# First-layer expert weights in pieces of 512 rows by 512 columns, in a one-core layer with attention, a recurrence and 32 experts

## The chip, the cores and the metric

The kernel runs on one core of one Trainium2 chip. Five engines of the core appear in the profile: PE (TensorE, the matrix multiplier; PEld is its weight load, which overlaps the matmuls), DVE (VectorE), ACT (ScalarE), POOL (GpSimd) and SP (SyncE, which here only issues DMA transfers). The metric is the device time of one execution in microseconds (us); less is better.

## The reference, cut to what matters

One transformer layer on 1024 tokens of width 1024: a layer norm, a mixing block (latent attention beside a recurrence), another norm, and then a mixture of 32 experts, four per token. The change touches only the first matrix product of the experts.

```python
def clamped_swiglu(hh):
    x_glu = jnp.minimum(hh[..., ::2], SWIGLU_LIMIT)
    x_lin = jnp.clip(hh[..., 1::2], -SWIGLU_LIMIT, SWIGLU_LIMIT)
    return x_glu * jax.nn.sigmoid(SWIGLU_ALPHA * x_glu) * (x_lin + 1.0)

def expert_block(args):          # idx: the tokens of one expert e
    idx, e = args
    u = clamped_swiglu(h_pad[idx] @ w1[e] + b1[e])   # w1[e] is 1024 x 2048
    return u @ w2[e] + b2[e]                         # w2[e] is 1024 x 1024
```

The output of each expert is multiplied by the token's gate and added to the token's row.

## The kernel before

**Two kinds of experts.** The experts are ranked by their number of tokens, and each rank has a fixed capacity: 192, 184, 184, 176, 168, 160, 152, 152, 144, 144 and 136 slots for the eleven largest (the wide ones), and 128 for the other 21 (the narrow ones). They run in the order narrow, wide, narrow, wide, narrow, narrow, wide, narrow, narrow, wide and so on, so most of the program repeats a period of two narrow experts and one wide one.

**Three products for one.** Weights and activations are float32. Each is split into a rounded high part and a low part that holds the rest: an ACT cast writes the high part (`wsh`, L205), and a DVE subtraction writes the low part (`wsl`, L206). A product is then three matmuls in `mm`: high by high (L193), high part of the weights' side by low part of the other and the reverse (L194, L195).

**Pieces.** `piece` (L1378) loads 1 MB of weights as a tile of 128 partitions by 2048, by one DMA on SP's queue, and splits it in two halves of 1024 columns: two casts on ACT, and two subtractions on DVE. The loaded tiles `w` have five buffers, the split tiles `ws` four. One expert takes 12 pieces, eight for the first layer and four for the second. In the kernel before, a piece of the first layer holds all 1024 rows (eight blocks k of 128) of 256 columns.

**The narrow first layer** (`first`): the tokens `xT` stand on PE's stationary side, and the weights stream through. For each quarter q of the 2048 columns an accumulator `acc` of 128 x 512 gets a bias matmul (L1472) and then two pieces: piece j fills columns j * 256 to j * 256 + 255, by 8 blocks k of three matmuls of 256 columns each. Then ACT takes the sigmoid (L1482) and DVE the rest (L1484 to L1486).

**The wide first layer** (`first_wide`): here the weights are stationary, 128 x 128 at a time, and the tokens `xw` stream through. A group is one 128-column block of the weights, summed over k: for each k one matmul of the high part of the weights by high and low tokens side by side, 2 * cap columns (L1525), and one of the low part by the high tokens, cap columns (L1527). An expert has 16 groups, two per piece. A group's accumulator is drained by ACT (L1529: the half of the low tokens, plus the bias) and DVE (L1530: the sum of both halves). The drains are called T0 to T15 in what follows, and the subtractions of piece j are called S j. After each second group, ACT and DVE do the activation (L1534 to L1537) and split the result `u` for the second layer.

**Banks.** The accumulators `acc` rotate through four PSUM banks, so group g of a wide expert waits until the drain T(g-4) has emptied its bank.

**What sets the order.** The whole program is written in one pass, and a scheduler that simulates the engines puts each engine's instructions in a fixed order at build time. Each engine then runs its list strictly in that order, so an instruction that stands behind another one waits for it even if they have nothing to do with each other. The order of the matmuls of two groups can be interleaved by the scheduler.

## Time and profile before

| what | value |
|---|---|
| time, median of 3 runs | 2455.2 us (2453.6 to 2470.61) |
| time of the profiled execution | 2466.53 us |
| its span from first to last instruction | 2464.7 us |
| mean granted TensorE clock | 0.954 |
| PE busy over the span | 2286.7 us, 93% |
| DVE busy over the span | 1996.8 us, 81% |
| ACT busy over the span | 1409.1 us, 57% |
| DMA, mean over the span | 230 GB/s |

The rows that are shown below come from the profiled execution, which took 2466.53 us; its span, 2464.7 us, is what the trace covers. Times in the rows are microseconds from the start of the span. The experts run from 957 us to the end.

### The profile page before, as it was taken

Reading aid. Unit: us, or ns where it says so; the run is one execution under the profiler, and the core shown is the slowest. Engines: PE = TensorE matmul, PEld = TensorE weight load, DVE = VectorE, ACT = ScalarE, POOL = GpSimd, SP = SyncE. Lnnn points to the kernel's source line nnn. Section 1 sums busy time; section 2 is a strip of 40 time slices with the busy share of each in tenths; the row PEclk is TensorE's granted clock in tenths of the full one; section 3 lists DMA queues with packets and bytes.
Section 4 is the critical chain, followed back from the end, with each engine's and each line's share of the span. In section 5 each row is a group of like instructions: output and inputs, shape, how many; then the busy total and the mean of one; then the engine's idle time right before and its main releaser. Section 6 shows DMA issues by size and latency. Waiting matters only on the chain. (4 is left out here: it accounts for less than half of the span.)

```text
span 2464.7 us, 42046 instructions
## 1 busy us (share of the span) xinstructions
PE 2286.7 (93%) x15539; PEld 1940.2 (79%) x15539; DVE 1996.8 (81%) x3878; ACT 1409.1 (57%) x2355; POOL 549.3 (22%) x411
## 2 busy tenths in 40 slices
PE   6999989999998995899999999999999999999992
PEld 3776766676765784888898998989889898888981
DVE  7666447777776776788898989898989898898977
ACT  5333335455545433666676767676667676666764
POOL 1005222222213533121211212111212121111113
PEclk9999989999898995999999999999999999999996
DMA  6378542212123323978898979897979898888973
GB/s 268 119 263 278 187 112 56 59 45 58 34 41 90 115 96 128 342 283 290 297 335 296 338 288 337 281 358 275 363 252 336 297 334 302 292 326 300 333 272 139
DMA packets 167335, 567.80 MB, mean 230 GB/s; under 512 B 64617, under 2 KB 79738, under 8 KB 116821
## 3 DMA queue, kind: packets, MB, share of 16 engines
q1 hardware_dynamic: 155476, 524.63, 58.2%
q0 software_dynamic: 11216, 39.34, 6.5%
q8 instruction: 124, 2.03, 0.3%
q10 hardware_dynamic: 432, 1.09, 0.1%
q14 instruction: 87, 0.70, 0.1%
HBM read 508.22 MB, written 56.79 MB: 229 GB/s over the span
## 5 line engine op out<-in xcount | busy, mean ns | idle before, releaser
L206 DVE TENSOR_TENSOR wsl<-w,wsh 128x1024 fp32r<-128x1024 f32 x786 | 932.9, 1218 | 143.6 <-ACT wsh L205 142.1
L205 ACT CAST wsh<-w 128x1024 fp32r<-128x1024 f32 x786 | 782.8, 1047 | 346.6 <-PE acc L195 91.9
L193 PE MATMUL acc<-wsh,xTh 128*128 128x256 f32 x1344 | 381.9, 285 | 10.0 <-ACT xTh L205 5.1
L1525 PE MATMUL acc<-xw,wsh 128*128 128x368 f32 (+7 forms) x1408 | 381.1, 354 | 8.0 <-DVE t L1530 8.0
L194 PE MATMUL acc<-wsl,xTh 128*128 128x256 f32 x1344 | 382.9, 285 | 0.7 <-DVE wsl L206 0.7
L195 PE MATMUL acc<-wsh,xTl 128*128 128x256 f32 x1344 | 381.7, 285 | 0.3 <-DVE xTl L206 0.3
L1527 PE MATMUL acc<-xw,wsl 128*128 128x184 f32 (+7 forms) x1408 | 337.9, 240 | 0.0
L1525 PEld LDWEIGHTS acc<-xw,wsh 128*128 128x128 f32 x1408 | 268.9, 191 | 10.1 <-issue 5.4
L1527 PEld LDWEIGHTS acc<-xw,wsl 128*128 128x128 f32 x1408 | 273.3, 194 | 0.7
L193 PEld LDWEIGHTS acc<-wsh,xTh 128*128 128x128 f32 x1344 | 258.5, 193 | 13.2 <-ACT xTh L205 7.0
L194 PEld LDWEIGHTS acc<-wsl,xTh 128*128 128x128 f32 x1344 | 259.4, 193 | 4.8 <-DVE wsl L206 1.0
L195 PEld LDWEIGHTS acc<-wsh,xTl 128*128 128x128 f32 x1344 | 259.2, 193 | 1.8 <-DVE xTl L206 0.6
L1459 POOL DMA_INDIRECT y_d<-y,idx x42 | 143.0, 3405 | 420.5 <-DVE y L1451 333.3
L1362 POOL DMA_INDIRECT xg<-h_d,idx x43 | 97.7, 2273 | 615.7 <-issue 272.2
L193 PE MATMUL acc<-wsh,uTh 128*128 128x512 f32 x512 | 203.5, 400 | 19.2 <-ACT uTh L205 19.2
L194 PE MATMUL acc<-wsl,uTh 128*128 128x512 f32 x512 | 202.4, 396 | 0.0
L195 PE MATMUL acc<-wsh,uTl 128*128 128x512 f32 x512 | 193.6, 406 | 1.3 <-DVE uTl L206 1.3
L193 PEld LDWEIGHTS acc<-wsh,uTh 128*128 128x128 f32 x512 | 97.3, 190 | 40.7 <-ACT uTh L205 21.8
L193 PE MATMUL sm<-hTh,wsh 128*128 128x512 f32 x288 | 115.0, 400 | 6.4 <-ACT wsh L205 2.0
L194 PE MATMUL sm<-hTl,wsh 128*128 128x512 f32 x288 | 115.6, 401 | 4.2 <-DVE hTl L347 3.1
L195 PE MATMUL sm<-hTh,wsl 128*128 128x512 f32 x288 | 113.5, 395 | 0.0
L194 PEld LDWEIGHTS acc<-wsl,uTh 128*128 128x128 f32 x512 | 97.8, 191 | 19.3 <-DVE wsl L206 0.2
(584 smaller groups left out, 4323.5 us busy)
## 6 DMA issues: line engine op xcount, KB each, us to landing
w<-in_w_dram SPq DMA_DIRECT2D x384, 1024.0 KB
aw<-in_ada_dram SPq DMA_DIRECT2D x34, 512.0 KB
w<-in_w_in_dram SPq DMA_DIRECT2D x18, 512.0 KB
aw<-in_ada_dram SPq DMA_DIRECT2D x7, 1024.0 KB
rkv_d<-stage SPq DMA_DIRECT2D x12, 512.0 KB
xt<-in_x_dram SPq DMA_DIRECT2D x8, 512.0 KB
xr<-in_x_dram SPq DMA_DIRECT2D x8, 512.0 KB
xr_d<-xr SPq DMA_DIRECT2D x8, 512.0 KB
```

Source lines behind the costliest of these rows:

```text
L193: mm(out, a.hi, b.hi, start=start, stop=False)
L194: mm(out, a.hi, b.lo, start=False, stop=False)
L195: mm(out, a.lo, b.hi, start=False, stop=stop)
L205: (hi_eng or self.nc.scalar.copy)(dst.hi, src)
L206: (lo_eng or self.nc.vector).tensor_tensor(dst.lo, src, dst.hi.bitcast(F32), ALU.subtract)
L1362: self.nc.gpsimd.indirect_dma_start(out=xg[0:n], out_offset=None, in_=self.h2_d, in_offset=bass.IndirectOffsetOnAxis(ap=idx[0:n, 0:1], axi ...
L1459: nc.gpsimd.indirect_dma_start(out=self.y_d, out_offset=bass.IndirectOffsetOnAxis(ap=idx[0:n, 0:1], axis=0), in_=y[0:n], in_offset=None, c ...
L1525: nc.tensor.matmul(acc[:, 0:2 * cap], w.hi[:, c], xw[:, k].rearrange("p a t -> p (a t)"), start=(k == 0), stop=False)
L1527: nc.tensor.matmul(acc[:, 0:cap], w.lo[:, c], xw[:, k, 0], start=False, stop=(k == KD - 1))
```

## The change

The same 1 MB pieces of the first layer are cut another way: 512 rows (four blocks k) by 512 columns. The host's layout of `w1` follows, so that a piece is still one contiguous block.

- In the narrow first layer a quarter q still takes two pieces, but each piece m now adds four blocks k to all 512 columns of the accumulator: 12 matmuls of 512 columns per piece, where there were 24 of 256.
- In the wide first layer a group sums over all eight blocks k, so it needs both pieces of a pair. Two pieces are loaded and split together at every even j, and then the four column blocks of the pair are summed one by one, each over both pieces. The number and the sizes of the matmuls stay.

```diff
--- before.py
+++ after.py
@@ -140,8 +140,8 @@
     o["rw"] = f("router_w")[0].reshape(KD, P, NE).transpose(1, 0, 2)
     o["rb"] = f("router_b")
 
-    w1 = f("exp_w1")[0].reshape(NE, KD, P, 8, P, 2)
-    o["w1"] = w1.transpose(0, 3, 2, 1, 5, 4).reshape(NE, 8, P, KD, 256)
+    w1 = f("exp_w1")[0].reshape(NE, 2, 4, P, 4, 2, P, 2)
+    o["w1"] = w1.transpose(0, 4, 1, 3, 2, 5, 7, 6).reshape(NE, 8, P, 4, 512)
     o["w2"] = f("exp_w2")[0].reshape(NE, 4, 2, P, D).transpose(0, 1, 3, 2, 4)
     b1 = f("exp_b1")[0].reshape(NE, 8, P, 2).transpose(0, 1, 3, 2)
 
@@ -1470,12 +1470,11 @@
         for q in range(4):
             acc = pm.tile([P, 512], F32, name="acc", bufs=4)
             nc.tensor.matmul(acc, self.pick[:, q:q + 1].to_broadcast([P, P]), bs, start=True, stop=False)
-            for j in range(2):
-                ws = self.piece(w1[bass.ds(e, 1), 2 * q + j].rearrange("o p k n -> (o p) (k n)"))
-                for k in range(KD):
-                    w, c = ws[k // 4], k % 4 * 256
-                    self.mm(acc[:, j * 256:(j + 1) * 256], xT[:, k], w[:, c:c + 256],
-                            start=False, stop=(j == 1 and k == KD - 1))
+            for m in range(2):
+                ws = self.piece(w1[bass.ds(e, 1), 2 * q + m].rearrange("o p k n -> (o p) (k n)"))
+                for k in range(4):
+                    c = k % 2 * 512
+                    self.mm(acc, xT[:, 4 * m + k], ws[k // 2][:, c:c + 512], start=False, stop=(m == 1 and k == 3))
             a = acc.rearrange("p (j g f) -> p j g f", j=2, g=2)
             v2 = lambda t: t.rearrange("p (j f) -> p j f", j=2)
             sg = mp.tile([P, 256], F32, name="sg")
@@ -1515,13 +1514,17 @@
         n1 = cap - P
         w1 = self.i["w1"]
         for j in range(KD):
-            ws = self.piece(w1[bass.ds(e, 1), j].rearrange("o p k n -> (o p) (k n)"))
+            if j % 2 == 0:
+
+                ws = []
+                for m in range(2):
+                    ws += self.piece(w1[bass.ds(e, 1), j + m].rearrange("o p k n -> (o p) (k n)"))
             parts = []
             for g in range(2):
                 acc = pm.tile([P, 512], F32, name="acc", bufs=4)
+                a = j % 2 * 2 + g
                 for k in range(KD):
-                    w = ws[k // 4]
-                    c = slice(k % 4 * 256 + g * P, k % 4 * 256 + (g + 1) * P)
+                    w, c = ws[k // 2], slice(k % 2 * 512 + a * P, k % 2 * 512 + (a + 1) * P)
                     nc.tensor.matmul(acc[:, 0:2 * cap], w.hi[:, c], xw[:, k].rearrange("p a t -> p (a t)"),
                                      start=(k == 0), stop=False)
                     nc.tensor.matmul(acc[:, 0:cap], w.lo[:, c], xw[:, k, 0], start=False, stop=(k == KD - 1))
```

After the diff, lines from L1483 to L1485 on stand one line higher, and lines from L1520 on three lines lower: the wide matmuls L1525 and L1527 become L1528 and L1530, and the drains L1529 and L1530 become L1532 and L1533.

PE, the first quarter of a narrow expert's first layer, behind the end of the expert ahead of it (L1435 and L1439); `pick` and `bs1` are the operands of the bias. Before:

```order
L1439 MATMUL acc_13276<-wsl_13356,u1_8914 64x512
L1435 MATMUL acc_13276<-wsh_13355,u1_8914 128x512
L1472 MATMUL acc_13408<-bs1_8920,pick_8916 128x512
L193 MATMUL acc_13408<-wsh_13412,xTh_13238 128x256
L194 MATMUL acc_13408<-wsl_13413,xTh_13238 128x256
L195 MATMUL acc_13408<-wsh_13412,xTl_13239 128x256
L193 MATMUL acc_13408<-wsh_13412,xTh_13238 128x256
```

And now:

```order
L1439 MATMUL acc_12796<-wsl_12876,u1_8914 64x512
L1435 MATMUL acc_12796<-wsh_12875,u1_8914 128x512
L1472 MATMUL acc_12928<-bs1_8920,pick_8916 128x512
L193 MATMUL acc_12928<-wsh_12932,xTh_12758 128x512
L194 MATMUL acc_12928<-wsl_12933,xTh_12758 128x512
L195 MATMUL acc_12928<-wsh_12932,xTl_12759 128x512
L193 MATMUL acc_12928<-wsh_12932,xTh_12758 128x512
```

The bias matmul stays, and the three matmuls of a block k are twice as wide; a piece is used up after 12 matmuls, where it took 24.

DVE in the wide first layer of an expert with 152 slots: `wsl` is S (each row without x2 is one half of a piece), L1530 is T, L1535 to L1537 the activation, `uTl` and `u1` the splitting of its result. Before:

```order
L206 TENSOR_TENSOR wsl_20839<-w_20836,wsh_20838 128x1024
L1537 SCALAR_TENSOR_TENSOR t1_20596<-sg_20599,t1_20596 128x152
L206 TENSOR_TENSOR wsl_20839<-w_20836,wsh_20838 128x1024
L1530 TENSOR_TENSOR t1_20653<-acc_20636,t1_20653 128x152
L1530 TENSOR_TENSOR t0_20690<-acc_20673,t0_20690 128x152
L206 TENSOR_TENSOR uTl_20436<-t1_20596,uTh_20435 128x128
L206 TENSOR_TENSOR u1_8914<-t1_20596,u1_8914 128x24
L1535 TENSOR_SCALAR t1_20653<-t1_20653 128x152
```

And now, where T is L1533, from the end of the activation of groups 4 and 5 on (`x2` stands for both halves of a piece):

```order
L206 TENSOR_TENSOR u1_8914<-t1_19164,u1_8914 128x24
L206 TENSOR_TENSOR wsl_19342<-w_19339,wsh_19341 128x1024 x2
L206 TENSOR_TENSOR wsl_19350<-w_19347,wsh_19349 128x1024 x2
L1533 TENSOR_TENSOR t1_19213<-acc_19196,t1_19213 128x152
L1533 TENSOR_TENSOR t0_19258<-acc_19241,t0_19258 128x152
L1533 TENSOR_TENSOR t1_19278<-acc_19261,t1_19278 128x152
```

The last three rows are T7, T8 and T9. Further down DVE's list of the same expert, with the second layer's first two pieces as `wsl_19495` and `wsl_19515`:

```order
L1540 SCALAR_TENSOR_TENSOR t1_19278<-sg_19281,t1_19278 128x152
L206 TENSOR_TENSOR wsl_19495<-w_19492,wsh_19494 128x1024 x2
L1533 TENSOR_TENSOR t0_19307<-acc_19290,t0_19307 128x152
L206 TENSOR_TENSOR uTl_18996<-t1_19213,uTh_18995 128x128
L206 TENSOR_TENSOR u1_8914<-t1_19213,u1_8914 128x24
L206 TENSOR_TENSOR wsl_19515<-w_19512,wsh_19514 128x1024 x2
L206 TENSOR_TENSOR uTl_18996<-t1_19278,uTh_18995 128x128
L206 TENSOR_TENSOR u1_8914<-t1_19278,u1_8914 128x24
L1533 TENSOR_TENSOR t0_19372<-acc_19355,t0_19372 128x152
L1533 TENSOR_TENSOR t1_19327<-acc_19310,t1_19327 128x152
L1533 TENSOR_TENSOR t1_19392<-acc_19375,t1_19392 128x152
```

Before, one piece's two subtractions stand between two pairs of drains. Now four subtractions (S6 and S7) stand in front of the drain of the last group of a pair (`t1_19213`, which is T7). In front of T11 (`t1_19327`) stand four of the second layer, with T10 and T12 (`t0_19307`, `t0_19372`) between and behind them.

PE, the third group of the same expert. Before, groups 2 and 3 read one piece, `wsh_20496`; the rows in front of the first line are second-layer matmuls of the expert ahead:

```order
L195 MATMUL acc_20339<-wsh_20407,uTl_19986 128x512
L1525 MATMUL acc_20502<-xw_20290,wsh_20496 128x304
L1527 MATMUL acc_20502<-xw_20290,wsl_20497 128x152
L1525 MATMUL acc_20502<-xw_20290,wsh_20496 128x304
L1527 MATMUL acc_20502<-xw_20290,wsl_20497 128x152
```

And now, from the fourth block k on:

```order
L1528 MATMUL acc_19062<-xw_18850,wsh_18999 128x304
L1530 MATMUL acc_19062<-xw_18850,wsl_19000 128x152
L1528 MATMUL acc_19062<-xw_18850,wsh_19007 128x304
L1530 MATMUL acc_19062<-xw_18850,wsl_19008 128x152
L1528 MATMUL acc_19062<-xw_18850,wsh_19007 128x304
L1530 MATMUL acc_19062<-xw_18850,wsl_19008 128x152
```

The third group takes its fifth block k from the pair's second piece, `wsh_19007`, which before was read by groups of its own.

## Rows read from the trace of the kernel before

**Rows 1.** Busy time of each engine in one period: two narrow experts, one wide.

```profile
core 0: us, PE busy (x) PEld busy (x) DVE busy (x) ACT busy (x) POOL busy (x), PEclk, DMA share, GB/s
1319.40:1346.60 27.20, 27.20 (x214) 26.45 (x213) 27.20 (x35) 21.01 (x27) 7.22 (x1) 1.00 0.96 348
1346.60:1393.60 47.00, 45.90 (x326) 41.09 (x325) 46.33 (x65) 32.86 (x43) 13.68 (x4) 1.00 0.93 348
1393.60:1432.00 38.40, 38.40 (x282) 37.91 (x280) 35.67 (x73) 26.66 (x54) 3.55 (x2) 1.00 0.83 292
1432.00:1451.00 19.00, 19.00 (x94) 14.84 (x93) 13.25 (x26) 9.74 (x16) 2.94 (x2) 1.00 0.61 227
sum 131.60, PE 130.50 PEld 120.28 DVE 122.45 ACT 90.27 POOL 27.40; mean PE 32.63 PEld 30.07 DVE 30.61 ACT 22.57 POOL 6.85
```

**Rows 2.** Waits of PE while the experts run, 957 to 2465 us: total, times, longest.

```profile
PE acc L193 <- ACT uTh L205: 19.2, 11, 6.1
...
PE acc L1525 <- DVE t L1530: 8.0, 8, 2.0
PE acc L193 <- ACT xTh L205: 5.1, 8, 0.6
```

**Rows 3.** Groups by form, 1100 to 2400 us: busy us, mean ns | idle before.

```profile
L206 DVE TENSOR_TENSOR wsl<-w,wsh 128x1024 fp32r<-128x1024 f32 x700 | 827.1, 1213 | 101.5 <-ACT wsh L205 100.1
L205 ACT CAST wsh<-w 128x1024 fp32r<-128x1024 f32 x700 | 696.6, 1047 | 272.4 <-PE acc L195 91.1 <-PE acc L1435 68.1 <-PE acc L1525 57.4
```

**Rows 4.** PE's timeline: 512-column matmuls 0 and 22, 256-column matmuls 0 and 23.

```profile
1301.32 0.39 PE L194 MATMUL acc<-wsl,uTh 128*128 128x512 f32 x1
...
1306.31 0.40 PE L195 MATMUL acc<-wsh,uTl 128*128 128x512 f32 x1
...
1319.64 0.28 PE L193 MATMUL acc<-wsh,xTh 128*128 128x256 f32 x1
...
1322.40 0.28 PE L195 MATMUL acc<-wsh,xTl 128*128 128x256 f32 x1
```

**Rows 5.** PE's timeline in the first narrow expert; in brackets the idle time before.

```profile
996.96 0.58 PE L193 MATMUL acc<-wsh,xTh 128*128 128x256 f32 x1 [4.94 <-ACT wsh L205]
```

**Rows 6.** PE's timeline, wide group of 152 slots: blocks k 0 and 8.

```profile
1935.98 0.34 PE L1525 MATMUL acc<-xw,wsh 128*128 128x304 f32 x1
...
1937.98 0.34 PE L1525 MATMUL acc<-xw,wsh 128*128 128x304 f32 x1
```

**Rows 7.** DVE's timeline in a narrow expert: both halves of a piece together.

```profile
1363.86 2.36 DVE L206 TENSOR_TENSOR wsl<-w,wsh 128x1024 fp32r<-128x1024 f32 x2 [0.51 <-ACT wsh L205]
```

**Rows 8.** DVE's timeline ahead of one late drain, then PE's, wide expert of 152 slots.

```profile
1814.74 1.22 DVE L206 TENSOR_TENSOR wsl<-w,wsh 128x1024 fp32r<-128x1024 f32 x1
1815.87 0.53 DVE L1530 TENSOR_TENSOR t<-acc,t 128x152 f32<-128x152 f32 x2
...
1816.33 0.50 PE L1525 MATMUL acc<-xw,wsh 128*128 128x304 f32 x1 [2.01 <-DVE t L1530]
```

**Rows 9.** DVE by form in a wide first layer of 152 slots, 1921.3 to 1957.6.

```profile
L1530 DVE TENSOR_TENSOR t<-acc,t 128x152 f32<-128x152 f32 x13 | 3.7, 306 | 0.0
L1536 DVE SCALAR_TENSOR_TENSOR t<-t,t 128x152 f32<-128x152 f32 x6 | 1.9, 313 | 0.1
...
L206 DVE TENSOR_TENSOR uTl<-t,uTh 128x128 fp32r<-128x128 f32 x5 | 1.4, 280 | 0.0
...
L206 DVE TENSOR_TENSOR xTl<-tr,xTh 128x512 fp32r<-128x512 f32 x2 | 1.4, 679 | 0.0
L1326 DVE TENSOR_TENSOR oh<-csts,pos 128x1024 bf16<-128x1024 f32 x1 | 1.2, 1212 | 0.0
L206 DVE TENSOR_TENSOR u<-t,u 128x24 fp32r<-128x24 f32 x5 | 0.9, 174 | 0.0
```

**Rows 10.** Stretches around the wait of rows 8, the granted clock third from the end.

```profile
1815.00:1817.00 2.00, 0.67 (x3) 0.70 (x4) 1.97 (x7) 0.81 (x4) 0.00 (x0) 0.86 0.92 365
1817.00:1819.00 2.00, 2.00 (x10) 2.00 (x10) 1.86 (x9) 1.26 (x5) 0.00 (x0) 0.50 0.71 270
1819.00:1820.50 1.50, 1.50 (x11) 1.50 (x11) 0.00 (x0) 0.43 (x1) 0.00 (x0) 0.72 0.92 371
1820.50:1822.00 1.50, 1.50 (x15) 1.50 (x14) 0.85 (x1) 1.50 (x3) 0.00 (x0) 1.00 0.19 76
```

## The prediction, made before the changed kernel ran

> **What bounds the kernel now.** I read the busy times by stretch first. In one period of two narrow experts and a wide one PE is busy 130.5 of 131.6 us, DVE 122.45, ACT 90.27 [rows 1]. PE sets the time, but DVE is a close second, and unevenly: in the first two stretches (the narrow experts) it is busy 73.53 of 74.2 us, in the last two (the wide one) 48.92 of 57.4. The slack of DVE lies in the wide stretch.
>
> Next the waits of PE: it waited 19.2 us for the second layer's input `u`, 5.1 us for a first input and 8.0 us for a drain of a wide group's bank (L1530), these in 8 waits [rows 2]. So PE loses little, and what the change can gain is PE work, or these few waits. The DMA queue moves 348 GB/s at a share of 0.96 and 0.93 in the narrow stretches [rows 1], but PE waits for no weights there. The groups by form show where DVE and ACT wait: the subtractions for the casts (101.5 us idle), and the casts for matmuls that free the split buffers [rows 3]. So DVE and ACT run as far ahead of PE as the four split buffers let them, and the pace comes from PE.
>
> **Narrow experts: fewer, wider matmuls.** Matmuls of 512 columns start 22 intervals apart at 1301.32 and 1306.31, so 0.2268 us each; of 256 columns 23 intervals apart at 1319.64 and 1322.40, so 0.1200 us each [rows 4]. Two of 256 take 0.2400 us and one of 512 takes 0.2267 us: 13.3 ns less for each matmul that goes. An expert has 4 quarters x 2 pieces x 8 blocks x 3 = 192 of them, 21 narrow experts 4032; 2016 go. 2016 x 13.3 ns = 26.9 us. The first narrow expert waits for its weights anyway, 4.94 us once [rows 5], so I count 20 experts: 25.6 us.
>
> The new matmuls read another operand than the measured ones of 512 (`xTh` for `uTh`), but the same sizes and the same three-part pattern; I know no row for them. The bound is 0 gain if they took 0.24 us; the nearest row says 0.2268.
>
> On this price the Trainium skill differs: "TensorE: Matmul & The Clock Gate", section "Wait — 56ns, not 53.3ns?", gives a fixed cost of about 2.5 ns per matmul at the full clock, by which 2016 fewer would save an estimated 5 us. The trace shows 13.3 ns of it at either width [rows 4], and the trace decides.
>
> **Whether DVE lets PE have it.** The two narrow experts of a period would take PE 2.6 us less, and DVE's work there stays at 73.53 us against 74.2 - 2.6 = 71.6. So DVE lacks 1.9 us per period, which it must have done ahead in the wide stretch, where it has 8.5 us of slack. Bounds over 10 periods: 0, if the split buffers hold that much lead, and 19 us, if they hold none. A piece of the first layer lasts PE 24 x 0.12 = 2.9 us and four buffers stand, so a lead of 1.9 us fits in them; I take 3 us, near the lower end.
>
> **Wide experts: the drains fall behind four subtractions.** The number of wide matmuls stays, and a group still takes 2.0 us at 152 slots [rows 6]. What moves is when split buffers come free. Before, a piece's buffer is free after its two groups; now both buffers of a pair after its fourth group, so ACT and DVE get their next two pieces at once. In the new order on DVE, S6 and S7 (four subtractions) stand ahead of T7, and four second-layer ones ahead of T11, where two stood between drains. Four take some 4.6 us: two together took 2.36 [rows 7], at a mean of 1.213 [rows 3]. Group 11 cannot start before T7, nor group 15 before T11.
>
> I walked this through for 152 slots, from the end of group 3 (time 0, where pair 0's buffers come free). S4 and S5 end at 4.95 (a cast of 1.05 ahead [rows 3], one short wait, four subtractions). T3 to T5 at 0.26 each (two in 0.53 [rows 8]) end at 5.75, six activation steps of 0.23 to 0.31 [rows 9] at 7.4, T6 at 7.65, the splitting of `u` and of the next input (two `xTl` of 0.68, two of 0.28, two of 0.17 [rows 9]) at 9.65. PE ends groups 4 to 7 at 8.0, so pair 1's buffers come free; casts run from there, behind ACT's own activation work, from 9.2 to 13.0; S6 and S7 end at 14.75, T7 at 15.0. PE has ended groups 8 to 10 at 14.0, and group 11 starts at 15.1: a wait of 1.1 us. Groups 11 to 14 then end at 23.3, with a wait of 0.2 for T10. On DVE T8, T9, six steps and a one-hot row of 1.21 [rows 9] end at 18.65, and four second-layer subtractions, T10, T12 and two splittings put T11 at 24.8. Group 15 starts at 24.9, after 1.6 us of waiting. Sum 2.9 us for one expert.
>
> By the same walk with each expert's own order and group length (2.25 us at 184 slots): 3.4 us at 192 slots, 0.6 and 0 at 184, 1.3 at 176, 1.8 at 168, 3.4 at 160, 2.9 twice at 152, 3.0 twice at 144, 2.0 at 136; together 24.3. Longer groups give the drains more time, which is why 184 comes off light. The 8.0 us that PE waits for drains now [rows 2] are replaced by these: +16.3 us. The bounds: -8.0 if DVE keeps up everywhere, and 11 x 5 = 55 if each expert waits for the whole four subtractions (4.6) and more.
>
> **The clock behind a wait.** After the wait of 2.01 us at 1816.33 [rows 8] the granted clock is 0.50 from 1817 to 1819 and 0.72 to 1820.5, the lower of the two levels (1.2 GHz) before it is back at 2.4 [rows 10]. PE loses 0.50 x 2.0 + 0.28 x 1.5 = 1.4 us there, and some 0.2 in the stretch ahead: about 1.55. Of the waits of the walk some six reach 1.5 us in one piece; 6 x 1.55 = 9.3, less two such drops that the drain waits cause now, 3.1: +6.2. Bounds: -3 and +31 (two drops in ten experts).
>
> **Start of a wide expert.** Group 0 needs the pair's second piece after four blocks k, where before it was needed only at group 2, some 4 us later. The bound above is one piece's two subtractions, 2.36 us [rows 7], in each of 11 experts, 26 us; below 0, since DVE is ahead there and PE's list has second-layer matmuls of the expert ahead between the first groups. I take 2.
>
> **DMA.** Still 1 MB per piece, contiguous, on the same queue, 12 per expert, in the same number of bytes; the issue is tied to the five `w` buffers, which free with the casts. A pair's casts wait together, so its loads do too, but PE waits for none of them now; 0, and if that cover is gone the price shows up as waits of the casts for `w`.
>
> **Sum.** -25.6 + 3 + 16.3 + 6.2 + 2 = +1.9 us. The rows come from the profiled execution of 2466.53 us, 0.46% above the median of 2455.2; the sum is a difference, so I set it on the median: **2457 us**, no change that a measurement can tell (I take 1%, 24.6 us, as the bound of that: 2430.6 to 2479.8).
>
> **Rivals.**
> (a) *Slower: the batches starve PE.* Each wide expert waits about 5 us in all (both T7 and T11 late by two subtractions more than I walked, 2.36 / 2 each) and drops the clock twice: 11 x (5 + 2 x 1.55) = 89 less the 8 + 3 of now and the 25.6 gained would be 2508; half of that cost, with one drop, 11 x (4 + 1.55) = 61 - 11 - 25.6 + 5, is +29: 2484 to 2490. It decides from the point where PE's extra waiting and its drops pass some 50 us. For it: in the trace a drain already came 2 us late behind two subtractions [rows 8]. Against: DVE has 8.5 us of slack in a wide stretch. The Trainium skill has the shape of this in "Perfetto Trace Analysis", section "Optimization Strategy": a gap that repeats on the engine that should be saturated can mean too few buffers for the next tile. By that rule a pair that holds two of four buffers would make one in every expert; the trace before shows such gaps only now and then [rows 2].
> (b) *Faster: pairing costs nothing.* DVE catches up in its slack, waits stay at 8 us: 2455.2 - 25.6 = 2430, or 2426 if the drain waits go too. For it: drains were late before as well, and PE waited only 8.0 us. Against: the new order on DVE.
> (c) *DVE is the bound in the narrow stretch*: of the 25.6 us 19 do not arrive, the rest as in the sum: 2457 + 16 = 2473.
> (d) *The change of width brings less*: at half the 13.3 ns, 13 us less gain: 2470.
>
> **How the numbers follow.** The forecast's case, with (c) and (d) as its upper edge, 0.62, of which 0.02 passes 2480; (a) 0.25; (b) 0.13. By the bound: faster 0.13, same 0.60, slower 0.27. The range leaves out at most the worse half of (a) and the outer part of (b): 2432 to 2490.
>
> **What the changed profile would show.** Narrow matmuls of 512 columns start 0.227 us apart, and a narrow expert lasts PE about 1.3 us less. PE's waits for the wide drains (L1533 there) rise from 8 to some 24 us, at groups 11 and 15, with subtractions on DVE ahead of them, and more stretches at clock 0.50 behind. If PE waits for `wsl` in narrow experts, (c) holds. The forecast is wrong if PE's waits for drains stay below 10 us, or pass 45.

## The result and the profile after

The changed kernel takes 2476.17 us (median of 20 runs, 2470.64 to 2483.17), the kernel before 2456.65 us in the same series (20 runs). The ratio is 1.0069, with a 95% interval of 1.0056 to 1.0081: slower by 0.7%, some 17 us by the ratio and 19.5 us by the medians. That lies in the range of the prediction and within 1%, but it is clear of noise, and 19 us above the forecast of 2457.

The profiled execution of after took 2478.02 us, close to its median; that of before, 2466.53 us, lies 10 us above its own. So the two traces differ by 11 us, and they are read here by stage. Four groups of rows of before have their answer.

Waits of PE while the experts run, 957 to 2480 us, kernel after (total, times, longest), beside [rows 2]:

```profile
PE acc L193 <- ACT uTh L205: 27.6, 19, 5.4
PE acc L195 <- DVE uTl L206: 13.5, 12, 1.7
PE tr L1330 <- DVE uTl L206: 10.6, 9, 1.2
...
PE tr L1374 <- DMA xg<-h_d,idx: 7.1, 1, 7.1
...
PE acc L1528 <- DVE t L1533: 3.5, 1, 3.5
...
PE acc L193 <- ACT xTh L205: 0.8, 1, 0.8
...
PE acc L194 <- DVE wsl L206: 0.5, 1, 0.5
```

One more line of before, PE's waits for gathered tokens (`xg`), 957 to 2465 us:

```profile
PE tr L1374 <- DMA xg<-h_d,idx: 12.3, 3, 7.9
```

The waits for wide drains, forecast to rise from 8.0 to 24 us, are down to one of 3.5. In their place PE waits for the two parts of `u`, the input of a second layer: 27.6 and 13.5 us, and 10.6 more where a one-hot matmul stands behind a late `uTl`. For the low part of a weight (`wsl`) it waits 0.5 us in all.

Stretches of PE, DVE and ACT in kernel after, beside [rows 1]: first from the start of a narrow expert that follows a wide one to the start of the next wide expert (the narrow stretch from here on), then the wide one:

```profile
1860.86:1939.17 78.31, 72.53 (x348) 58.42 (x347) 73.91 (x99) 53.46 (x71) 11.05 (x6) 0.98 0.92 342
1939.17:1994.16 54.99, 54.97 (x367) 49.83 (x367) 46.90 (x98) 36.37 (x69) 5.48 (x4) 1.00 0.75 263
```

The same two stretches cut the same way in kernel before:

```profile
1846.54:1921.26 74.72, 72.85 (x538) 67.37 (x537) 73.61 (x98) 53.67 (x71) 21.07 (x5) 1.00 0.94 348
1921.26:1975.95 54.69, 54.69 (x373) 49.99 (x370) 46.85 (x98) 36.63 (x69) 6.40 (x4) 1.00 0.78 270
```

The narrow stretch is 3.6 us longer, with PE idle for 5.8 us of it; the wide stretch is as long as it was. Over the trace, by the starts of the experts' first matmuls: the nine narrow stretches of two experts take 678.1 us before and 699.9 after (+21.8), the eleven wide ones 636.9 and 623.3 (-13.6). Of the 13.6 us some 4.5 are drain waits that are gone. Another 4.4 are two waits for gathered tokens that stood in wide stretches before (2.66 and 1.75 us, among the 12.3), and the rest comes mostly from clock drops behind both kinds of wait: four in the wide stretches before, one after. Before, six of the nine narrow stretches take 74.0 to 74.7 us and three 76.6 to 78.4, each of these with a wait of 2.2 to 3.0 us for `uTh` and a clock drop; after, two take 74.5 and seven 78.3 to 79.5.

PE's timeline in kernel after, a narrow expert behind a wide one: two high-by-low matmuls 15 apart, then the joint of its first and second layer:

```profile
1879.77 0.39 PE L195 MATMUL acc<-wsh,xTl 128*128 128x512 f32 x1
...
1883.17 0.39 PE L195 MATMUL acc<-wsh,xTl 128*128 128x512 f32 x1
1883.40 0.68 PE L1374 MATMUL tr<-csts,u 128*128 128x128 f32 x4
1885.96 0.50 PE L193 MATMUL acc<-wsh,uTh 128*128 128x512 f32 x1 [1.88 <-ACT uTh L205]
...
1888.85 1.22 PE L195 MATMUL acc<-wsh,uTl 128*128 128x512 f32 x2 [1.70 <-DVE uTl L206]
```

The new matmuls start (1883.17 - 1879.77) / 15 = 0.2267 us apart, as priced [rows 4], and such a first layer lasts 22.7 to 23.0 us where it lasted 24.1. But the transposes of `u` (L1374) now come after the last of them, all four at once, and PE has nothing else in its list until `uTh` is there. ACT's and DVE's timelines at that place say why it is late:

```profile
1883.64 1.99 ACT L205 CAST wsh<-w 128x1024 fp32r<-128x1024 f32 x2 [0.48 <-PE acc L195]
1885.54 0.36 ACT L205 CAST uTh<-tr 128x256 fp32r<-128x256 f32 x1
...
1886.12 2.34 DVE L206 TENSOR_TENSOR wsl<-w,wsh 128x1024 fp32r<-128x1024 f32 x2
1888.39 0.41 DVE L206 TENSOR_TENSOR uTl<-tr,uTh 128x256 fp32r<-128x256 f32 x1
```

The cast of `u` stands behind two weight casts, its subtraction behind two weight subtractions, all for pieces that PE does not need yet: by the order of the subtractions, DVE ends a piece of this first layer 2.5 to 3.8 us before PE's first matmul with its low part. The same place in kernel before, PE's and then ACT's timeline:

```profile
1864.98 0.38 PE L1374 MATMUL tr<-csts,u 128*128 128x128 f32 x2
1870.47 0.40 PE L193 MATMUL acc<-wsh,uTh 128*128 128x512 f32 x1
...
1866.69 0.37 ACT L205 CAST uTh<-tr 128x256 fp32r<-128x256 f32 x1
```

There the first transposes stand inside the first layer, 5.5 us ahead of the first use, and the cast is done 3.4 us ahead.

The clock behind such a wait, stretches of kernel after, beside [rows 10]:

```profile
1752.00:1755.42 3.42, 1.19 (x4) 0.67 (x4) 3.42 (x6) 1.03 (x4) 0.00 (x0) 1.00 1.00 414
1755.42:1758.92 3.50, 3.50 (x8) 2.76 (x9) 1.94 (x6) 0.00 (x0) 0.00 (x0) 0.52 1.01 414
```

Two waits in a row (1.88 and 1.70 us) leave PE at a granted clock of 0.52, next to its lower level of 1.2 GHz, for 3.5 us, which costs 1.7 us. The clock falls at this place in seven of the nine narrow stretches (in two of them behind waits of 1.77 and 0.7 us, and for twice as long); in the first two, where no wait is longer than 1.2 us, the stretch takes 74.5 us and the clock stays.

### The profile page after: what moved, and what is told of

The parts are those of the page before. It is cut to its first block, busy times and chain, and to the rows that moved or that the text cites. A ratio compares the mean times of both kernels' runs of the same rounds, so it can differ in the third digit from the quotient of the medians.

```text
span 2475.9 us, 38049 instructions
## 1 busy us (share of the span) xinstructions
PE 2270.6 (92%) x13523; PEld 1829.5 (74%) x13523; DVE 1994.4 (81%) x3878; ACT 1406.6 (57%) x2353; POOL 471.6 (19%) x411
## 3 DMA queue, kind: packets, MB, share of 16 engines
q8 instruction: 108, 1.77, 0.3%
## 4 chain that ended last, share of the span: by engine, by line
PE 33%; DVE 20%; issue 5%; ACT 2%; DMA 1%; SPq 0%; POOLq 0%; POOL 0%; DVEq 0%; ACTq 0%
DVE wsl L206 14%; PE acc L1528 10%; PE acc L195 6%; PE acc L193 5%; PE acc L194 5%; PE acc L1530 4%; ACT wsh L205 1%; DMA w<-in_w_dram 1%; PE tr L1374 1%; PE acc L1439 1%; PE acc L1435 1%; DVE ln L1483 1%; DVE uTl L206 1%; DVE oh L1326 1%; DVE y L1451 1%
## 5 line engine op out<-in xcount | busy, mean ns | idle before, releaser
L1528 PE MATMUL acc<-xw,wsh 128*128 128x368 f32 (+7 forms) x1408 | 373.8, 350 | 3.5 <-DVE t L1533 3.5
L1530 PE MATMUL acc<-xw,wsl 128*128 128x184 f32 (+7 forms) x1408 | 334.2, 239 | 0.0
L1530 PEld LDWEIGHTS acc<-xw,wsl 128*128 128x128 f32 x1408 | 269.5, 192 | 0.4
L1528 PEld LDWEIGHTS acc<-xw,wsh 128*128 128x128 f32 x1408 | 264.9, 189 | 4.6 <-issue 3.7
L193 PE MATMUL acc<-wsh,xTh 128*128 128x512 f32 x672 | 263.6, 395 | 5.1 <-ACT wsh L205 4.2
L194 PE MATMUL acc<-wsl,xTh 128*128 128x512 f32 x672 | 264.7, 394 | 0.5 <-DVE wsl L206 0.5
L195 PE MATMUL acc<-wsh,xTl 128*128 128x512 f32 x672 | 264.1, 393 | 0.0
L193 PE MATMUL acc<-wsh,uTh 128*128 128x512 f32 x512 | 208.0, 409 | 27.6 <-ACT uTh L205 27.6
L195 PE MATMUL acc<-wsh,uTl 128*128 128x512 f32 x512 | 201.6, 418 | 13.6 <-DVE uTl L206 13.5
L1459 POOL DMA_INDIRECT y_d<-y,idx x42 | 114.3, 2722 | 501.7 <-DVE y L1451 386.3
L1362 POOL DMA_INDIRECT xg<-h_d,idx x43 | 54.9, 1276 | 623.3 <-DVE xTl L206 222.8
L193 PEld LDWEIGHTS acc<-wsh,xTh 128*128 128x128 f32 x672 | 127.4, 190 | 31.9 <-ACT wsh L205 4.5
L194 PEld LDWEIGHTS acc<-wsl,xTh 128*128 128x128 f32 x672 | 127.5, 190 | 27.8 <-DVE wsl L206 1.0
L195 PEld LDWEIGHTS acc<-wsh,xTl 128*128 128x128 f32 x672 | 127.3, 189 | 27.0 <-DVE xTl L206 0.2
L195 PEld LDWEIGHTS acc<-wsh,uTl 128*128 128x128 f32 x512 | 96.9, 197 | 40.6 <-DVE uTl L206 21.9
```

What stands on the lines that cost most here:

```text
L193: mm(out, a.hi, b.hi, start=start, stop=False)
L194: mm(out, a.hi, b.lo, start=False, stop=False)
L195: mm(out, a.lo, b.hi, start=False, stop=stop)
L1362: self.nc.gpsimd.indirect_dma_start(out=xg[0:n], out_offset=None, in_=self.h2_d, in_offset=bass.IndirectOffsetOnAxis(ap=idx[0:n, 0:1], axi ...
L1459: nc.gpsimd.indirect_dma_start(out=self.y_d, out_offset=bass.IndirectOffsetOnAxis(ap=idx[0:n, 0:1], axis=0), in_=y[0:n], in_offset=None, c ...
L1528: nc.tensor.matmul(acc[:, 0:2 * cap], w.hi[:, c], xw[:, k].rearrange("p a t -> p (a t)"), start=(k == 0), stop=False)
```

## The experiments

Three theories went in. **Theory 1, order:** the splitting of `u` stands behind weight splitting in the lists of ACT and DVE. **Theory 2, VectorE:** DVE is the bound of the narrow stretch, so PE's shorter matmuls cannot arrive there (rival (c) of the prediction). **Theory 3, pairs:** the pairing of split buffers costs in the wide experts (the forecast's own main term). All stretches below are narrow stretches, in the columns of [rows 1]. The kernel before was run again beside each group of experiments, with medians of 2461.5 to 2463.7 us; the ratios are to these, while the expected times rest on some 2455.

**Each half of the change alone.** The host keeps both layouts; `first` or `first_wide` takes the new one.

```diff
+    w1s = f("exp_w1")[0].reshape(NE, 2, 4, P, 4, 2, P, 2)
+    o["w1s"] = w1s.transpose(0, 4, 1, 3, 2, 5, 7, 6).reshape(NE, 8, P, 4, 512)
...
-        w1 = self.i["w1"]
+        w1 = self.i["w1s"]
```

Narrow experts only:

> Only the narrow experts take pieces of 512 rows by 512 columns; the wide ones keep 1024 by 256 (both layouts of the weights lie in memory). Theory 1 (order): the loss of the change sits in the narrow expert behind a wide one, where the casts and subtractions that split u now stand behind the second layer's weight splitting. Here that order is nearly the one of before (the first u transposes have 14 matmuls of 512 columns, 3.2 us, behind them), so the 25 us of shorter matmuls arrive: 2427 to 2438 us, and from the start of a narrow expert behind a wide one to the next wide expert 71.5 us, where it took 74.0 before. Theory 2 (VectorE is the bound in the narrow stretch): VectorE's work there is unchanged, so that stretch stays at 73.5 to 74 us, PE waits for wsl, and the time is 2450 to 2457. Theory 3 (split buffers that come free in pairs cost in the wide experts): as theory 1, since no pair is left.

Measured: 2483.89 us, ratio 1.0077 (1.0050 to 1.0104). All three theories had it at 2457 or less, and all are wrong on the total. One of its better narrow stretches, of nine that take 73.8 to 83.4 us:

```profile
2009.30:2084.26 74.96, 71.31 (x349) 57.09 (x347) 73.65 (x99) 53.63 (x71) 50.52 (x5) 1.00 0.93 348
```

PE's work fell, DVE's 73.65 us did not, and the stretch took 1.3 us more than DVE's work: near theory 2's floor, but PE's waits in it are for `u` (2.24 us for `uTl`, 0.91 for `uTh`) and not for `wsl`, as theory 2 had it. Over all experts waits for gathers, `uTl` and drains (19.0, 16.9 and 11.0 us, with eleven clock drops between 1100 and 2400 us) came on top. The order near the end of the first layer, which theory 1 had called good, did not save it.

Wide experts only:

> Only the wide experts take the new pieces in pairs; the narrow ones keep 1024 by 256. Theory 1 (order): the pairing alone already puts the first splitting of u behind three of the second layer's four weight casts, and leaves 14 matmuls of 256 columns (1.7 us) behind the first u transposes where 44 (5.3 us) stood; so PE waits for uTh or uTl in the narrow expert behind each wide one, 1 to 3 us a period, 2460 to 2485 us, and the wide experts themselves stay as long as they were. Theory 2 (VectorE is the bound): the same VectorE work, no change, 2452 to 2460. Theory 3 (pairs): 2470 to 2490 with the waits at the wide groups' drains or at the casts, and a longer wide stretch (over 58 us at 152 to 176 slots).

Measured: 2467.18 us, ratio 1.0018 (1.0000 to 1.0036), which by itself cannot be told from theory 2's "no change"; the stretches decide. In its trace the eleven wide ones take 623.4 us, as in the whole change: the pairing costs nothing there, and theory 3 is out. That the pairing gains the 13 us is not shown: two kernels further down whose wide experts are unpaired, the kernel before and the narrow-only one with subtractions on GpSimd, take 622.4 and 621.4 us in theirs. Its narrow stretches, with untouched code, take 694.0 us, 16 more than before:

```profile
1991.35:2068.97 77.62, 74.94 (x541) 68.57 (x539) 74.32 (x99) 53.48 (x71) 11.36 (x6) 0.98 0.91 341
```

PE's waits in it are all for `u`, in the expert behind the wide one: 0.47 and 1.41 us for `uTl`, 0.79 for `uTh`. So with an edit of the wide experts alone the splitting of `u` in the narrow ones moved and cost them a little more than the wide ones took less: theory 1's place, and its size.

**Order put back by hand.** In the whole change, the weight splits of four pieces of a narrow expert are queued behind parts of the activation or of the splitting of `u`: two pieces behind one instruction each, two behind the cast and the subtraction of a part of `u` (the expectations count these as five edges).

```diff
-            self.split(ws[:, slice(*c)], w[:, slice(*c)])
+            with ExitStack() as st:
+                for i in after or ():
+                    st.enter_context(self.tc.issue_after(i.ins))
+                self.split(ws[:, slice(*c)], w[:, slice(*c)])
...
+                        after = {1: self.gs[1:2], 2: self.done[0], 3: self.done[1]}.get(q) if isinstance(u, Split) else None
+                        ws += self.piece(w2[bass.ds(e, 1), q].rearrange("o p k n -> (o p) (k n)"), after)
...
+                ws = self.piece(w1[bass.ds(e, 1), 2 * q + m].rearrange("o p k n -> (o p) (k n)"), self.gs[0:1] if (q, m) == (3, 1) else None)
...
+            self.gs.append(V.scalar_tensor_tensor(u[:, q * 256:(q + 1) * 256], sg, SIG7, ln, ALU.min, ALU.mult))
...
+                self.done.append(self.flip(uT, u, 2 * q - 2, 2 * q))
```

> The whole change, and in narrow experts five issue-order edges and no wait: the split of the first layer's last piece stands behind the activation of the first quarter, the second layer's second piece behind the activation of the second quarter, its third and fourth pieces behind the splitting of the first and second part of u. Nothing is computed otherwise. 11 matmuls of 512 columns (2.5 us) then stand behind the first u transposes. Theory 1 (order): the 5.1 us of waits and 1.6 us of low clock per period shrink to under 2, so 2432 to 2448 us. Theory 2 (VectorE is the bound): VectorE has the same work in another order, PE waits for wsl instead, 2465 to 2480. Theory 3 (pairs): the pairs are still there, 2470 to 2480.

Measured: 2464.72 us, ratio 1.0014 (0.9998 to 1.0031); its narrow stretches sum to 687.2 us, 13 less than in the whole change. With the first-layer edge one piece earlier, `(q, m) == (3, 0)`:

> As the kernel with five edges, but both pieces of the first layer's last quarter stand behind the activation of the first quarter, so that 23 matmuls of 512 columns (5.2 us, what the kernel before had) stand behind the first u transposes. Theory 1 (order): as good as that kernel or up to 8 us faster, 2428 to 2446. Theory 2 (VectorE is the bound) and theory 3 (pairs): 2465 to 2480.

Measured: 2472.72 us, ratio 1.0049 (1.0027 to 1.0070), stretches 697.4 us. A stretch of each, the first kernel, then the second:

```profile
1862.26:1938.97 76.71, 72.32 (x348) 58.40 (x347) 73.83 (x99) 53.62 (x71) 11.74 (x6) 0.98 0.95 348
```

```profile
1858.71:1936.60 77.89, 73.40 (x349) 59.00 (x347) 73.97 (x99) 53.62 (x71) 10.25 (x6) 0.96 0.94 343
```

The order is worth some 13 us of the loss, but neither kernel comes to theory 1's 2448 or less, and both lie at or near the range of 2465 to 2480 that theories 2 and 3 gave. At its first use of `u` PE waits in none of the nine stretches of either kernel. DVE is busy for 73.8 us again, and PE waits elsewhere: in the first kernel 2.6 to 3.3 us in every stretch, ahead of a one-hot matmul, for the `uTl` of a later part of the same expert's `u`. So the edges moved the wait more than they removed it.

**Two subtractions per narrow expert on GpSimd.** This was to give DVE 4.8 us of room per stretch.

```diff
-            self.split(ws[:, slice(*c)], w[:, slice(*c)])
+            self.split(ws[:, slice(*c)], w[:, slice(*c)], lo_eng=lo if c[0] else None)
...
+                ws = self.piece(w1[bass.ds(e, 1), 2 * q + m].rearrange("o p k n -> (o p) (k n)"), lo=G if q % 2 == 1 and m == 0 else None)
```

> The changed kernel with 2 of the 24 subtractions of each narrow expert (the second half of the first pieces of quarters 1 and 3) on GpSimd, so VectorE has 4.8 us less work from a narrow expert behind a wide one to the next wide expert. Theory 2 (VectorE is the bound there: its busy time over that stretch was 73.1 to 74.0 us in every kernel so far, whatever PE's work and the order): VectorE falls to about 69 us, PE's 71.5 becomes the bound, the stretch takes 71.5 to 73.5 us, and the time is 2428 to 2445. Theory 1 (order alone, VectorE has room): the stretch stays where the better order of the five edges left it, 74.5 to 77 us, 2455 to 2470.

> The kernel before with the same two subtractions of each narrow expert on GpSimd. Theory 2 (VectorE is the bound in the narrow stretch): PE is the next bound there, at 72.9 us busy with 256-column matmuls, so at most 1.1 us per period are to be had: 2443 to 2457, 10 to 25 us slower than the changed kernel with the same relief. Theory 1 (order alone): no less than 2452, and within 10 us of the changed kernel with the relief.

> Only the narrow experts with pieces of 512 by 512, and the same two subtractions of each on GpSimd. Theory 2: without the relief this kernel took 2484 with VectorE busy 73.7 us of 75; with it the narrow stretch takes 71.5 to 73.5 us and the time falls by 20 us or more, to 2430 to 2460 (the waits for drains in its wide experts, 1.8 us each with a drop of the clock, may stay). Theory 1 (order alone): 2470 to 2485, since its order was already near that of before.

Measured, whole change: 2479.05 us, ratio 1.0074 (1.0047 to 1.0102). Kernel before: 2454.71, ratio 0.9974 (0.9956 to 0.9992). Narrow experts only: 2450.96, ratio 0.9960 (0.9942 to 0.9977). The relief did not take place, so these say nothing for or against theory 2. The whole change lies outside both theories' ranges; that narrow-only lies in theory 2's 2430 to 2460 is luck, since its stretches take 74.9 to 78.4 us and not 71.5 to 73.5. A stretch of the whole change with it, then GpSimd's and DVE's timelines in that stretch:

```profile
1863.07:1939.88 76.81, 70.97 (x348) 57.16 (x347) 76.81 (x95) 53.94 (x71) 36.69 (x10) 1.00 0.94 334
```

```profile
1873.89 4.01 POOL L206 TENSOR_TENSOR wsl<-w,wsh 128x1024 fp32r<-128x1024 f32 x1
...
1875.61 3.37 DVE L206 TENSOR_TENSOR wsl<-w,wsh 128x1024 fp32r<-128x1024 f32 x1
```

DVE is busy for all of the 76.81 us with four instructions fewer: while GpSimd subtracts, a DVE subtraction of 1.2 us takes 3.37. (In the kernel before none of this size took more than 1.3 us between 1100 and 2400 us.) The Trainium skill says in "Perfetto Trace Analysis", section "Optimizing Scalar/DVE Operations", that the two engines share a read port, so that moving work between them might not help; the run agrees, with a loss on DVE of 2.2 us beside the 1.2 it was spared. That narrow-only became 33 us faster with it (29 by the ratios) is put down to its new order, which no run shows by itself: its wide stretches, where nothing was moved to GpSimd, fell from 638.7 to 621.4 us, its narrow ones from 691.7 to 682.7, and its waits for gathers from 19.0 to 7.9 us, for drains from 11.0 to 3.4.

**Two low parts per narrow expert left out.** Where DVE wrote the low part ACT writes a copy of the weights, so these low parts are missing and the result is not the reference's; the sizes and the number of PE's matmuls stay. ACT had 20 us of room in the stretch.

```diff
+        if lo_eng == "ACT":
+            self.nc.scalar.copy(dst.lo, src)
+            return
...
+                ws = self.piece(w1[bass.ds(e, 1), 2 * q + m].rearrange("o p k n -> (o p) (k n)"), lo="ACT" if q % 2 == 1 and m == 0 else None)
```

> The changed kernel, but the low part of the second half of two first-layer pieces in each narrow expert (first pieces of quarters 1 and 3) is left out: ACT copies the weights there in its place, a part of the result that is then not the reference's. VectorE has two subtractions less per narrow expert and GpSimd none more, ACT has 20 us of room in the stretch. With the subtractions on GpSimd the relief did not arrive: VectorE was busy for 76 us of the stretch with fewer instructions, single subtractions of 1.2 us lasting 3.4. Theory 2 (VectorE is the bound in the narrow stretch): VectorE falls to 68.5 to 70 us there, PE's 71.5 is the bound, the stretch takes 71.5 to 73.5 us, the time is 2430 to 2446. Theory 1 (order alone): the order of the u transposes is good here, as it was with the edges (2465) and with GpSimd (2479), and the stretch stays at 74.5 to 77: 2455 to 2475.

Measured: 2400.85 us, ratio 0.9763 (0.9731 to 0.9795), 75 us under the whole change. A narrow stretch:

```profile
1815.49:1885.66 70.17, 70.17 (x349) 57.36 (x347) 69.45 (x95) 57.30 (x74) 13.88 (x6) 1.00 0.97 364
```

With DVE at 69.45 us PE never waits, and the stretch is PE's own work, 70.17 us. Nine stretches sum to 633.2 us, 67 less than in the whole change. Theory 1's 2455 is far off, and theory 2's 2430 is 29 us too high as well, with 71.5 us or more for a stretch that takes 70.2. The order is another one too: 19 matmuls of the first layer stand behind the first transposes of `u` in every stretch, none in seven of the nine of the whole change. So the 67 us are room on DVE and a better order together.

> The kernel before with the same two low parts per narrow expert left out in favour of a copy on ACT. Theory 2: PE's 72.9 us busy is the next bound, so the stretch falls from 74.0 to 73 or 73.5 us and the time by 5 to 12 us, and the changed kernel with the same relief is 8 to 20 us faster than this one: the shorter matmuls pay once VectorE has room. Theory 1 (order alone): no change, and the changed kernel with the relief is no faster than this one.

Measured: 2478.74 us, ratio 1.0064 (1.0034 to 1.0095), against the expectation of theory 2. A stretch, and two of its waits over all experts:

```profile
1589.26:1665.67 76.41, 74.25 (x541) 68.76 (x539) 70.94 (x95) 57.19 (x74) 12.97 (x6) 0.98 0.96 346
```

```profile
PE acc L193 <- ACT uTh L205: 15.7, 16, 3.7
PE tr L1333 <- DVE uTl L209: 12.7, 9, 1.4
```

Here DVE has 5.5 us of room and PE still waits for `u`, 0.75 us for `uTh` and 1.41 for `uTl` in this stretch: the order costs without a bound on DVE, so room on DVE alone is not enough. More of the loss lies in the wide stretches, which no edit touched: they take 649.2 us (636.9 before), the narrow ones 686.3 (678.1), and PE waits for gathers for 19.2 us in all.

> Only the narrow experts with pieces of 512 by 512, and the same two low parts per narrow expert left out in favour of a copy on ACT. Theory 2: the narrow stretch falls from 75 to 71.5 to 73.5 us, 2430 to 2450, 30 us or more under the same kernel without the relief (2484). Theory 1 (order alone): its order was near that of before already, so 2465 to 2484.

Measured: 2407.40 us, ratio 0.9782 (0.9747 to 0.9818), a stretch of 70.2 us:

```profile
1817.32:1887.51 70.19, 70.19 (x348) 57.36 (x347) 69.38 (x94) 57.17 (x74) 17.86 (x6) 1.00 0.96 361
```

The narrow half by itself pays nearly as much as the whole change, once DVE has room and the order is the same good one (19 matmuls again). Theory 2's 2430 to 2450 was too high here too.

**One split per piece instead of two halves**, a smaller relief that leaves nothing out:

```diff
-CUT = ((0, 1024), (1024, 2048))
+CUT = ((0, 2048),)
```

> The whole change with the five issue-order edges, and each piece split by one cast and one subtraction of 2048 columns where it took two of 1024; nothing is left out. Two subtractions in a row take 2.36 us now, at 1.157 from start to start of which 1.067 is a column per 0.96 GHz-like pace by the two lengths, so one of 2048 should take about 2.27 and VectorE should save some 0.09 us per piece, 1.1 us per narrow expert: 71.5 us in the narrow stretch. Theory 2 (VectorE is the bound there, with a floor at its busy time, and PE's 70.2 us next): the stretch falls from 74.5 to 77 to 72 to 75 us, the time to 2435 to 2455. Against it: the whole piece is ready later, and waits for u may stay, 2455 to 2470.

> Only the narrow experts with pieces of 512 by 512, and each piece split by one cast and one subtraction of 2048 columns; nothing is left out. Here 22 matmuls of 512 columns stand behind the first u transposes or the second follow close, nearly as in the kernels with the relief on ACT. Theory 2: VectorE 71.5 us in the narrow stretch, the stretch takes 72 to 74 us, the time is 2435 to 2455, at least 25 us under the same kernel with split halves (2484). Theory 1 (order alone, no floor from VectorE): the good order gives 70.2 to 71 us in the stretch as in the kernel with the relief on ACT, 2405 to 2425.

Measured: with the edges 2492.26 us, ratio 1.0112 (1.0055 to 1.0170); narrow experts only 2460.80, ratio 0.9990 (0.9966 to 1.0015). A stretch of each:

```profile
1734.64:1813.28 78.64, 72.37 (x349) 58.30 (x347) 73.96 (x75) 51.34 (x48) 11.06 (x6) 0.98 0.94 348
```

```profile
1872.05:1944.42 72.37, 70.78 (x349) 57.19 (x347) 72.10 (x74) 51.67 (x48) 40.56 (x6) 1.00 0.96 358
```

The first lies above all ranges given for it, with PE waiting 3.53 us for a `uTl`, and does not show the floor. The second does: DVE 72.10, stretch 72.37, as theory 2 had it for the stretch, and all nine sum to 670.0 us, 8 less than before, with nothing left out. The total missed its 2435 to 2455, since its wide stretches take 636.6 us again and it waits 14.4 us for gathers, and two of its narrow stretches take 76.9 and 81.1 us. No kernel of this study that computes everything beats both by more than the 0.4% of narrow-only with GpSimd, which is put down to its order.

What speaks for a floor by DVE is that the shortest of the nine narrow stretches follows DVE's work over three levels of it:

| kernel | DVE's work in it, us | shortest narrow stretch, us |
|---|---|---|
| before | 73.3 | 73.96 |
| whole change | 73.2 | 74.45 |
| whole change with the edges | 73.1 | 74.54 |
| narrow only, one split per piece | 72.1 | 72.37 |
| whole change, low parts left out | 69.4 | 70.13, PE's own work |

The floor is inferred all the same. In none of these shortest stretches does PE wait for a weight's low part; where it waits, it is for `u` (before, also 0.6 us for a first input), which stands in line behind the weights. An order with `u` ahead of the weights everywhere and DVE's work whole was not found, so whether DVE could then let PE have more is open.

## Why the prediction was right on the time and not on the reason

The time was within the range and "no change within 1%" held, but by luck: the sum came near by terms that missed in both directions. By its own sign the forecast was wrong, since PE's waits for drains stayed below 10 us (3.5).

- **Shorter matmuls, -25.6: right as PE work.** 0.2267 us apart, and where nothing else stands in the way the narrow stretch is PE's 70.17 us, where PE was busy for 72.85. That is 2.7 us per stretch of two experts against 2.56 priced.
- **Whether DVE lets PE have it, +3 of 0 to 19: the term that was mis-sized.** DVE's work in the narrow stretch was 72.5 to 74.6 us in every kernel that left it whole, halves unmerged, and without GpSimd. It was 73.6 of 74.7 us already [rows 1 show 73.53 of 74.2 in another cut]; if that work is the floor, at most 1 us of the 2.6 could arrive. The shortest narrow stretch of the changed kernel is 74.45 us, against 73.96 before: none of the 25.6 us arrived. That DVE would do the missing 1.9 us ahead, in its slack of the wide stretch, did not happen, and the trace shows why no further lead can be built up there. ACT's and DVE's timelines at the end of a wide expert, 7 us before the next narrow one starts:

```profile
1987.19 3.90 ACT L205 CAST wsh<-w 128x1024 fp32r<-128x1024 f32 x4 [4.37 <-PE acc L1435]
```

```profile
1988.27 2.36 DVE L206 TENSOR_TENSOR wsl<-w,wsh 128x1024 fp32r<-128x1024 f32 x2 [5.14 <-ACT wsh L205]
```

The split buffers are full: ACT sits idle for 4.37 us until PE has used one up in the wide expert's second layer (L1435), and DVE for 5.14 us behind it. The lead that stands then, 3.8 us at the narrow expert's first piece, is still 2.5 to 3.8 us through its first layer, so it was not the weights that were late in the end. Room of 4.5 us on DVE, with the other order that came with it, released 67 us over nine stretches, more than the whole forecast gain, since the late `u` went with it.
- **The step that is missing: `u`.** The prediction followed the order at the wide drains and never read it at the joint of a narrow expert's two layers. There the transposes of `u` moved from inside the first layer to behind it, and their splits behind weight splits. In the stretch shown PE waits 1.88 + 1.70 + 0.66 + 1.18 + 0.37 = 5.8 us, all for `u`, and loses 1.7 to the clock: 78.3 us. In the changed kernel's own best, 74.45 us, the waits at the same places are 0.95 + 0.74 + 1.18 + 0.37 = 3.2 us and the clock stays. The hand-made order took back 13 us of 22; room on DVE with a better order all of it and 45 more.
- **Wide drains, +16.3: wrong, -13.6 with the clock.** The walk had T7 at 15.0 us after group 3 and group 11 ready at 14.0. The trace has the same four subtractions in front, but neither time. PE's and DVE's timelines in the second expert of 152 slots of kernel after, where group 3 ends at 1950.5:

```profile
1956.30 1.03 PE L1374 MATMUL tr<-csts,xg 128*128 128x128 f32 x8
...
1959.83 4.63 DVE L206 TENSOR_TENSOR wsl<-w,wsh 128x1024 fp32r<-128x1024 f32 x4 [0.40 <-ACT wsh L205]
1964.37 0.75 DVE L1533 TENSOR_TENSOR t<-acc,t 128x152 f32<-128x152 f32 x3
...
1965.45 0.38 PE L1528 MATMUL acc<-xw,wsh 128*128 128x304 f32 x1
```

The four subtractions do stand ahead of T7, which is done at about 1964.7, 14.2 us after group 3 and 0.8 earlier than in the walk. ACT's casts for them start at 1958.75, 8.25 us after group 3 where the walk had 9.2, and 0.6 us before PE's last matmul of group 7: the walk lets both buffers of a pair come free at the end of its fourth group, but the first piece is used up after that group's fourth block k. And PE had transposes of the next expert to do between groups 6 and 7 (1.03 us), so it reaches group 11 only at 1965.45, 15.0 us after group 3, and does not wait. 0.8 us on one engine and 1.0 on the other were the difference between a wait of 1.1 us and none. T11, which the walk had 24.8 us after group 3, is done at about 23 us, as PE comes to group 15. The 13.6 us that the wide stretches take less are half drains and half gathers, with their clock drops, and the prediction had no term for gathers.
- **Clock, +6.2, and start of a wide expert, +2.** Between 1100 and 2400 us the granted clock falls to 0.50 seven times in either trace, which costs 12.0 us before and 15.4 after, so +3.4. Before, four of the seven are in wide stretches; after, all are at `u`. A drop costs 1.7 us, not 1.55; the prediction's own rows give 1.00 + 0.42 + 0.28 = 1.70 [rows 10]. The start of a wide expert cost nothing that shows: at 160 slots the wide stretch is 55.67 us, 55.61 before.
- **Rivals.** (a) fell, and with it what the prediction had worked out by the Trainium skill's sentence on repeating gaps: the pairs of buffers made no gap that repeats in the wide experts. A gap that repeats came up at another place, behind `u`. (b) came true in the wide half alone. (c) gave 2473, next to the measured time, for half of the reason at most: the narrow stretch stayed at DVE's work or above, but its sign, PE waiting for `wsl`, did not come (0.5 us).

The two traces are 11.2 us apart: +21.8 in the narrow stretches, -13.6 in the wide ones, -2.4 in the three narrow experts outside them and the end, and +5.3 ahead of the first expert, in a part that no edit touches and that ends at 980 to 992 us in the traces of this study. The other 6 to 8 us of the measured difference lie within what one execution of before differs from its median and are not settled.

## What to carry to other kernels

Before a saving on the bounding engine is counted, look at the next engine in the same stretch: one that is busy for 99% of it may let no more than the last per cent through, and room elsewhere in the period does not help unless work can move there, which full buffers prevent. Where a scheduler sets the order, an edit moves instructions at places that it does not touch; read the order at every joint where a result of one layer feeds the next, above all how far ahead of its first use a small, late operand stands and what long instructions of the same engine stand in front of it. And a predicted wait of a microsecond needs the whole lists of both engines, since other work of that size, or a buffer that comes free half a group earlier, decides whether it exists. A gain in a stretch is put down to an edit only when kernels without the edit do not show it too.

## What the runs showed of the hardware that was not expected

A subtraction of 128 x 1024 on GpSimd, which took 2.9 to 4.7 us in the stretch shown, slowed one on DVE beside it from 1.2 to 3.37 us, so four subtractions moved away in a stretch raised DVE's busy time from 73.9 to 76.8 us. And one subtraction of 2048 columns took 2285 ns, against 2340 to 2360 for two of 1024 in a row: halving a piece costs DVE less than 0.1 us.
